# Weight blocks in one tile of five places, neighbours split together, and a fourth pair in blocks in the last down projections

## The chip, the cores and the metric

The kernel runs on one core of one Trainium2 chip. The metric is the device time of one execution in microseconds. A profile of one execution shows what each engine did: TensorE (PE, with its weight loads as PEld), VectorE (DVE), ScalarE (ACT), GpSimd (POOL) and SyncE (SP). SP, ACT and POOL also issue transfers.

## The reference

One layer of a decoder trunk on 256 rows of 2048 floats: a feed-forward block, a mixer (attention beside a matrix memory), an output projection, a second feed-forward block, and a last normalization. All weights are float32, and most of the work is matrix products with them.

```
x = x + 0.5 * swiglu(rmsnorm(x, ffn1_norm), ffn1_w_gate, ffn1_w_up, ffn1_w_down)
h = rmsnorm(x, mix_norm);  parts = split(h @ w_in)
y_a = diff_attention(...);  y_b = mlstm_chunkwise(...) * sigmoid(m_o)
x = x + concat(y_a, y_b) @ w_out
x = x + 0.5 * swiglu(rmsnorm(x, ffn2_norm), ffn2_w_gate, ffn2_w_up, ffn2_w_down)
out = rmsnorm(x, final_norm)
# swiglu(h, g, u, d) = (silu(h @ g) * (h @ u)) @ d ; hidden width 5632
```

## The kernel before, in words

**Products in split precision.** A weight block is cut into a high part `wh` (a cast on ScalarE, line 132) and a low part `wl` (weight minus high part, on VectorE, line 133). Activations are cut the same way. Each product of a 128x128 piece of activations and a 128x512 weight block is then three matmuls (`mms`): two with `wh` (lines 181 and 182) and one with `wl` (line 184). TensorE takes them in the order of the program.

**Pairs in blocks.** The 256 rows are two halves (`hb`). Weights come in tiles of 128 rows by 512 columns, taken in pairs (two tiles down, k and k+1) and, for two neighbouring column chunks `wa` and `wb`, as blocks of two by two. Plainly (`plain`) such a pair takes eight products. A pair "in blocks" takes seven, by a scheme of sums of blocks as in fast matrix multiplication: the class `Paired` does the first `ns` pairs of a product so, and the rest plainly. For each pair in blocks a raw tile of three slots holds the block of `wa` for k (slot 0) and the two of `wb` (slots 1 and 2); the fourth block comes later as `late`. The steps, by their names in the code:

- `leading`: for each two pairs (a "two"; the last may be alone): load, split slot 0 and multiply (A1); then on VectorE the sum T1 writes slots 0 and 1 (line 479). One step later, `second_sum`: split slot 0 and multiply (S1), then T2 adds slot 2 to slot 0: by an accumulating transfer on the POOL queue (line 495) where `by_dma` holds, there are more than three pairs in blocks and the two isn't the last; else on VectorE (line 497).
- `sums`: for each two, load the late block (line 511, SP queue), split slot 0 and multiply (S2), and add the late block to slot 0 by a transfer (line 533, POOL queue); then split and multiply the late blocks themselves (A2, `bare`); then slot 1 (S3).
- `second`: for each pair one split of slots 0 and 2 together (128x1024) for two products, and plain units of `wa` between.
- `third`: the last plain unit of `wa`, then the plain units of `wb`, one for each pair of `rest`. With `last_units` the second half's products of the last units are kept back to the end, so that the first half is finished earlier.

`Chain.run` weaves the leading steps of one product between the `third` steps of the one before.

**Buffers and order.** Raw tiles come from a pool of five (`wr`), plain pairs and late blocks from another five (`rawp`), and `wh` and `wl` from four each. Splits and loads have a high priority in the scheduler that orders each engine's queue; it follows the reads and writes of tiles. `split_weights` also keeps some hand-made order between splits and other work on ScalarE and VectorE. In a `Paired`, block loads go through the POOL queue (lines 446 and 208; SP for the first three chunks of an FFN), plain loads through SP (line 219).

**The feed-forward block.** `ffn` takes the hidden width in groups of 3, 2, 3 and 3 double chunks (`PARTS`). Each group does its gate and up products (5 pairs in blocks of 8; 3 in the second of the first FFN, whose first chunk is taken plainly), and then two down products (chunks 0 and 1, then 2 and 3), each with `NP_DOWN` pairs in blocks: 3, 2, 3 and 3 of 6, 4, 6 and 6. `by_dma` is off for all of them. Hidden pairs that are taken in blocks need their own sums (`sum_pair`, lines 343 to 345, and a split). The mixer's products have 2 pairs in blocks, then 3, 5, 5, 5 and 3; the output projection has two products of 3.

**The end.** The last down product finishes chunk 3 half by half in `store` (from line 1171): add to the residual (line 1181), square on ScalarE (line 300), the last factor (line 1192, POOL), scale (lines 1196 and 1198) and store (line 1199).

Of the kernel before, what the change touches and what calls it, by code (L numbers as in the profile page):

```python
# [9 lines left out]
F32 = mybir.dt.float32  # L10
# [7 lines left out]
P = 128  # L18
# [6 lines left out]
CW = 512  # L25
# [7 lines left out]
UK = 2  # L33
# [5 lines left out]
NP_FIRST = 3  # L39
FIRST_IN = 2  # L40
PARTS = (3, 2, 3, 3)
NP_DOWN = (3, 2, 3, 3)
LK = 4
AHEAD = 400
XLATE = 75
# [4 lines left out]
ON_POOL = 3  # L50
FIRST_SUMS = 3
FLUSH = 3

SEEDED = N11, N21 = "n11", "n21"

# [5 lines left out]
def tile_trunk_layer(ctx: ExitStack, tc: tile.TileContext, x, xt, par, bias_if, lamv, fnorm,  # L61
                     wg1, wu1, wd1, wqk0, wqk1, wqk2, win, wout, wg2, wu2, wd2, out):
    nc = tc.nc
# [1 line left out]
    big = ctx.enter_context(tc.tile_pool(name="big", bufs=1))  # L65
    slots = ctx.enter_context(tc.tile_pool(name="slots", bufs=22))
    work = ctx.enter_context(tc.tile_pool(name="work", bufs=8))
    wr = ctx.enter_context(tc.tile_pool(name="wr", bufs=5))
    wrp = ctx.enter_context(tc.tile_pool(name="wrp", bufs=5))
    wsp = ctx.enter_context(tc.tile_pool(name="wsp", bufs=4))  # L70
    small = ctx.enter_context(tc.tile_pool(name="small", bufs=2))
    ps_acc = ctx.enter_context(tc.tile_pool(name="ps_acc", bufs=4, space=PSUM))
    ps_tr = ctx.enter_context(tc.tile_pool(name="ps_tr", bufs=2, space=PSUM))

    wqk = [wqk0, wqk1, wqk2]
    uid = [0]

    def nm(s):
        uid[0] += 1
        return f"{s}_{uid[0]}"  # L80
# [47 lines left out]
        nc.vector.scalar_tensor_tensor(lo, src, prm[:, gcol:gcol + 1], hi.bitcast(F32),  # L128
                                       op0=ALU.mult, op1=ALU.subtract)

    def split(src, hi, lo):
        return (nc.scalar.copy(hi, src),  # L132
                nc.vector.tensor_tensor(out=lo, in0=src, in1=hi.bitcast(F32), op=ALU.subtract))  # L133


# [1 line left out]
    splits, queued = [], ([], [])  # L137

    def after(late, early):

        tc.add_manual_dep(late.ins, early.ins.name,
                          mybir.DependencyInfo(mybir.DependencyClass.NoSync, mybir.DependencyReason.DATA),
                          reason="order")
# [3 lines left out]

    ahead = ([], [])

    def split_weights(src, hi, lo):  # L150
        made = split(src, hi, lo)
        for late, q, past in zip(made, queued, ahead):
            while q and len(splits) >= q[0][0]:
                past.append(q.pop(0)[1])
            del past[:-3]
            for early in past:
                after(late, early)
        return made


    def pair_tiles(pool, tag, shape):
        return (pool.tile(shape, F32R, tag=tag + "h", name=nm(tag + "h")),
                pool.tile(shape, F32R, tag=tag + "l", name=nm(tag + "l")))
# [36 lines left out]
    def flush(n=None):  # L200

        now = pending[:n]
        del pending[:n]
        for f in now:
            f()

    def load_pair(dst, w, k, queue=nc.sync):
        queue.dma_start(dst, w[k // LK][:, k % LK:k % LK + 2, :])

    def load_unit(w, k, pieces=(UK,), spare=False):  # L210
        n = w.shape[3]
        if spare:
            raw = wr.tile([P, 3, n], F32, tag="raw", name=nm("raw"))[:, 0:UK, :]
        else:
            raw = wrp.tile([P, UK, n], F32, tag="rawp", name=nm("rawp"))
        with tc.high_priority(offset=AHEAD):
            o = k % LK
            for m in pieces:
                nc.sync.dma_start(raw[:, o - k % LK:o - k % LK + m, :], w[k // LK][:, o:o + m, :])
                o += m  # L220
        return raw
# [3 lines left out]
    def in_turn(load):  # L225
        for early in turns[-1:]:
            after(load, early)
        turns.append(load)

    def tile_by_tile(w, ahead):  # L230
        raw = wr.tile([P, 3, w.shape[3]], F32, tag="raw", name=nm("raw"))
        hi, lo = pair_tiles(wsp, "w", [P, UK, w.shape[3]])
        with tc.high_priority(offset=AHEAD):
            for t in range(UK):
                ahead(0, t)
                in_turn(nc.sync.dma_start(raw[:, t, :], w[0][:, t, :]))
                made = split_weights(raw[:, t, :], hi[:, t, :], lo[:, t, :])
        splits.append(made)
        ahead(1)
        return hi, lo  # L240

    def units(accs, xp, w, nk, last_units=1, ahead=None, w0=0, banks=None):
# [16 lines left out]
        for u in range(nu):  # L259
            if u == FLUSH:  # L260
                flush()
# [65 lines left out]
    A1, B1, A2, B2, S3, S1, S2, S4 = range(8)  # L327
# [60 lines left out]
    def gate(src, r):  # L388
        s = wk("sg")
        with soon():  # L390
            ahead_of_splits(0, nc.scalar.activation(s, src, AF.Silu, scale=r))
        return s
# [5 lines left out]
    def soon(extra=40):  # L398
        return tc.high_priority(offset=AHEAD + extra)

    class Early:


        def __init__(self, engine):
            self.engine = engine
# [16 lines left out]
    class Paired:  # L422

        def __init__(self, xp, wa, wb, nk, ns, w0=0, queue=nc.gpsimd, by_dma=True):

            self.queue, self.by_dma = queue, by_dma and ns > 3
            self.xp, self.wa, self.wb, self.k0 = xp, wa, wb, w0 * LK
            self.ns, self.rest = ns, range(2 * ns, nk, UK)
            self.twos = [range(j, min(j + 2, ns)) for j in range(0, ns, 2)]

            self.n = wa.shape[3]
            self.off = self.n - wb.shape[3]
            self.raws = []

        def job(self, acc, j, xi, w, wi, first, last, on=False):
            xh, xl = self.xp[j][2 * (xi // 4):][:2]
# [2 lines left out]

        def load(self, j):  # L440
            n, off = self.n, self.off
            raw = wr.tile([P, 3, n], F32, tag="raw", name=nm("raw"))
            self.raws.append(raw)
            k = self.k0 + 2 * j
            with tc.high_priority(offset=AHEAD):
                self.queue.dma_start(raw[:, 0, :], self.wa[k // LK][:, k % LK, :])
                load_pair(raw[:, 1:3, off:], self.wb, k, self.queue)
                if off:
                    nc.gpsimd.memset(raw[:, 1:3, 0:off], 0.0)

        def split_two(self, srcs):
# [7 lines left out]
                splits.append(made)  # L459
            return t  # L460

        def part(self, js, acc, xi, slot, first=False, last=False):

            t = self.split_two([self.raws[j][:, slot, :] for j in js])
            mms([self.job(acc, j, xi, t, i, first and j == 0, last and j == self.ns - 1, not first)
                 for i, j in enumerate(js)])

# [170 lines left out]
    def ffn(chain, xp, rstd, wg, wu, wd, finish, first=None):  # L638


        def inner(hid, c, ns):
            sg = []

            def half(ag):
                r = rstd()
                sg.extend(gate(ag[hb], r[:, hb:hb + 1]) for hb in range(NT))

            def end(au):
                r = rstd()
                with soon():  # L650
                    hs = [gated(au[hb], r[:, hb:hb + 1], sg[hb]) for hb in range(NT)]
                hid_transposes(hs, hid, c, ns)

            return half, end

        def add(c):
            def run(accs):
                for hb in range(NT):
                    if c % 2:
                        add_half(accs[hb], xres[:, hb, c * CW:(c + 1) * CW], 0.5)  # L660
                    else:
                        add_part(accs[hb], hb, c)

            return run

        done = 0
        for part, (n, ns) in enumerate(zip(PARTS, NP_DOWN)):
            hid = {}
            for c in range(n):
                half, end = inner(hid, c, ns)  # L670
                if done + c == 0 and first is not None:
                    half(linear(xp, wg[0], KD, ahead=first[0],
                                banks=[functools.partial(seeded, b) for b in (N11, N21)]))
                    au = []
                    stream = units(au, xp, wu[0], KD, banks=[bank, bank])
                    for i in range(KD // UK - NP):
                        next(stream)
                        if i < NP_FIRST - FIRST_IN:
                            first[1]()
                    chain.put(stream, NP, functools.partial(end, au))  # L680
                else:
                    np_, queue = NP, nc.sync if done + c < ON_POOL else nc.gpsimd
                    if done + c == 1 and first is not None:
                        np_ = NP_FIRST
                        pending.extend([first[1]] * (NP - NP_FIRST))
                    chain.run(Paired(xp, wg[done + c], wu[done + c], KD, np_, queue=queue), half, end)
            last = part == len(PARTS) - 1
            for c in (0, 2):
                p = Paired(hid, wd[c], wd[c + 1], n * 4, ns, done, by_dma=False)
                if last:  # L690
                    chain.run(p, functools.partial(finish, c), functools.partial(finish, c + 1),
                              LAST_UNITS if c else 1)
                else:
                    chain.run(p, add(c), add(c + 1))
            done += n
# [343 lines left out]
    for hb in range(NT):  # L1039
        for h in range(NH):  # L1040
            i = hb * NH + h
# [226 lines left out]
```

## Time and profile before

| | |
|---|---|
| median of 3 runs | 1759.46 us (1758.83 to 1760.01) |
| the profiled execution's own time | 1759.56 us |
| its span, first to last instruction | 1757.8 us |
| granted TensorE clock | 0.999 |
| instructions | 24486 |
| loads of raw blocks for the gate and up products on POOL | 80 of 256 KB, 80 of 512 KB |

The page gives for each engine its busy time and instructions. Views of the trace group the instructions by line, list waits with who ended them ("A <- B: us in total, times, longest"), follow the chain that ended last, and list instructions in order of time (start, length, engine, line, what is written and read, count).

### The profile page before, as it was taken

The page shows a single profiled execution, that of the slowest core. Times are in us where ns is not written, and L with a number is a line of the kernel's source. Part 1 is how long each engine was busy: PE and PEld are TensorE (multiplying, and loading weights), DVE is VectorE, ACT ScalarE, POOL GpSimd, SP SyncE. Part 2 cuts the span into 40 slices and gives each one's busy share as a digit, 9 for nine tenths or more (in the row PEclk, how much of TensorE's full clock was granted, in tenths as well). Part 3 has the DMA queues.
Part 4 walks back from the last instruction along what each step waited for, and adds up shares of the span by engine and source line. Part 5 has one row for each costly group of instructions (what it writes and reads, how often), then busy time and mean ns, then how long its engine had stood idle before and what let it go on. Part 6 is the DMA issues. An engine that isn't in the chain of part 4 may idle for free.

```text
span 1757.8 us, 24486 instructions
## 1 busy us (share of the span) xinstructions
PE 1744.6 (99%) x7926; PEld 1437.7 (82%) x7926; DVE 1617.8 (92%) x2189; ACT 1267.4 (72%) x1949; POOL 429.3 (24%) x630
## 2 busy tenths in 40 slices
PE   9999999999999999999999999999999999999998
PEld 7788888888888888987888888888888878888886
DVE  7999999999999999898888999999999999999997
ACT  8666777777677768777687777776777677677765
POOL 0022332322233312012231101122332332233310
PEclk9999999999999999999999999999999999999999
DMA  9787998999799977577886667898998999799973
GB/s 365 251 254 209 259 261 265 253 292 265 218 262 258 263 252 204 185 230 221 236 238 192 209 210 211 260 265 233 258 260 268 241 268 276 232 246 256 283 254 115
DMA packets 155265, 429.72 MB, mean 244 GB/s; under 512 B 17632, under 2 KB 18944, under 8 KB 154880
## 3 DMA queue, kind: packets, MB, share of 16 engines
q0 software_dynamic: 76304, 196.66, 45.1%
q1 hardware_dynamic: 77680, 229.40, 38.0%
q10 hardware_dynamic: 1152, 2.09, 0.3%
q8 instruction: 62, 1.02, 0.2%
q14 instruction: 67, 0.55, 0.1%
HBM read 349.56 MB, written 2.10 MB: 200 GB/s over the span
## 4 chain that ended last, share of the span: by engine, by line
PE 93%; DMA 2%; DVE 2%; issue 1%; ACT 0%; POOL 0%; SPq 0%; POOLq 0%; DVEq 0%; ACTq 0%
PE acc L184 18%; PE acc L181 18%; PE acc L182 18%; PE accn L181 12%; PE accn L182 12%; PE accn L184 12%; DVE wl L133 1%; DMA raw<-in_wg_dram 1%; PE tr L373 1%; DMA raw<-in_wu_dram 1%; PE tr L314 0%; PE sc L1060 0%; DMA rawp<-in_wg_dram 0%; ACT wh L132 0%; PE num L1011 0%
## 5 line engine op out<-in xcount | busy, mean ns | idle before, releaser
L132 ACT CAST wh<-raw 128x512 fp32r<-128x512 f32 (+2 forms) x885 | 601.5, 708 | 214.5 <-PE acc L182 66.3
L133 DVE TENSOR_TENSOR wl<-raw,wh 128x512 fp32r<-128x512 f32 (+2 forms) x885 | 676.1, 793 | 58.4 <-ACT wh L132 54.5
L132 ACT CAST wh<-rawp 128x1024 fp32r<-128x1024 f32 (+3 forms) x308 | 318.2, 1035 | 109.5 <-PE acc L182 55.1
L133 DVE TENSOR_TENSOR wl<-rawp,wh 128x1024 fp32r<-128x1024 f32 (+3 forms) x308 | 367.1, 1197 | 32.0 <-ACT wh L132 29.8
L181 PE MATMUL acc<-wh,xs 128*128 128x512 f32 (+2 forms) x956 | 369.5, 387 | 0.0
L182 PE MATMUL acc<-wh,xs 128*128 128x512 f32 (+2 forms) x956 | 368.9, 386 | 0.0
L184 PE MATMUL acc<-wl,xs 128*128 128x512 f32 (+2 forms) x956 | 317.6, 387 | 0.8 <-DVE wl L133 0.7
L533 POOL DMA_DIRECT2D raw<-late x176 | 152.6, 1053 | 442.7 <-DVE wl L133 422.9
L181 PE MATMUL acc<-wh,xt 128*128 128x512 f32 (+2 forms) x564 | 218.4, 388 | 0.7 <-ACT wh L132 0.7
L182 PE MATMUL acc<-wh,xt 128*128 128x512 f32 (+2 forms) x564 | 217.3, 386 | 0.0
L181 PE MATMUL accn<-wh,xt 128*128 128x512 f32 (+1 forms) x552 | 215.3, 391 | 0.0
L182 PE MATMUL accn<-wh,xt 128*128 128x512 f32 (+1 forms) x552 | 214.7, 390 | 0.0
L479 DVE TENSOR_TENSOR raw<-raw 128x1024 f32<-128x1024 f32 x176 | 211.0, 1217 | 0.8
L184 PEld LDWEIGHTS acc<-wl,xs 128*128 128x128 f32 x956 | 178.3, 188 | 39.2 <-DVE wl L133 3.6
L181 PEld LDWEIGHTS acc<-wh,xs 128*128 128x128 f32 x956 | 179.5, 188 | 36.4 <-ACT wh L132 0.6
L182 PEld LDWEIGHTS acc<-wh,xs 128*128 128x128 f32 x956 | 179.6, 188 | 35.6
L181 PE MATMUL accn<-wh,xs 128*128 128x512 f32 (+1 forms) x408 | 162.6, 400 | 1.9 <-ACT wh L132 1.9
L182 PE MATMUL accn<-wh,xs 128*128 128x512 f32 (+1 forms) x408 | 158.0, 388 | 0.0
L184 PE MATMUL acc<-wl,xt 128*128 128x512 f32 (+2 forms) x564 | 157.6, 386 | 0.0
L495 POOL DMA_DIRECT2D raw<-raw x92 | 78.9, 899 | 322.1 <-DVE wl L133 234.7
L184 PE MATMUL accn<-wl,xt 128*128 128x512 f32 (+1 forms) x552 | 154.7, 388 | 0.0
L184 PE MATMUL accn<-wl,xs 128*128 128x512 f32 (+1 forms) x408 | 140.9, 388 | 0.0
(229 smaller groups left out, 2125.0 us busy)
## 6 DMA issues: line engine op xcount, KB each, us to landing
rawp<-in_wd_dram SPq DMA_DIRECT2D x88, 512.0 KB, 5.6
raw<-late POOLq DMA_DIRECT2D x174, 256.0 KB, 5.3
raw<-in_wu_dram POOLq DMA_DIRECT2D x80, 512.0 KB, 8.4
rawp<-in_wu_dram SPq DMA_DIRECT2D x73, 512.0 KB, 5.1
rawp<-in_wg_dram SPq DMA_DIRECT2D x69, 512.0 KB, 5.2
raw<-raw POOLq DMA_DIRECT2D x92, 256.0 KB, 4.1
raw<-in_wd_dram POOLq DMA_DIRECT2D x44, 512.0 KB, 8.6
late<-in_wg_dram SPq DMA_DIRECT2D x41, 512.0 KB, 9.2
```

The lines of the kernel that those rows point to most:

```text
L132: return (nc.scalar.copy(hi, src), nc.vector.tensor_tensor(out=lo, in0=src, in1=hi.bitcast(F32), op=ALU.subtract))
L133: nc.vector.tensor_tensor(out=lo, in0=src, in1=hi.bitcast(F32), op=ALU.subtract))
L181: nc.tensor.matmul(acc, lh, rh, start=first, stop=False, skip_group_check=on)
L182: nc.tensor.matmul(acc, ll, rh, start=False, stop=False, skip_group_check=on)
L184: newest[:] = [nc.tensor.matmul(acc, lh, rl, start=False, stop=last, skip_group_check=on)]
L373: nc.tensor.transpose(tr[:, i, hb * P:(hb + 1) * P], hs[hb][:, k * P:(k + 1) * P], ident)
L479: nc.vector.tensor_tensor(out=raw[:, 0:2, :], in0=raw[:, 0:3:2, :], in1=raw[:, 1:2, :].to_broadcast([P, 2, n]), op=ALU.add)
L495: nc.gpsimd.dma_start(raw[:, 0, :], raw[:, 2, :], accum_op=ALU.add)
L533: nc.gpsimd.dma_start(self.raws[j][:, 0, :], lates[-1][1][:, i, :], accum_op=ALU.add)
```

## The change

Raw blocks no longer come as tiles of a pool, but as places in one tile `ring` of five, dealt in turn (`raw_place`), to `Paired.load` and to the two other users, `load_unit` with `spare` and `tile_by_tile`. Where a two lies in neighbouring places, `part` splits slot 0 (or 1) of both with one cast and one subtraction of 128x1024 (`split_both`); in A1 it makes two casts, one for each block, and one subtraction. Where it doesn't (places 4 and 0, or a lone pair), the split is as before. The last entry of `NP_DOWN` becomes 4, and `by_dma` is on in the last group's two down products of each FFN, so that T2 of their first two goes by transfer.

```
-NP_DOWN = (3, 2, 3, 3)
+NP_DOWN = (3, 2, 3, 4)
+RAWS = 5
...
-    wr = ctx.enter_context(tc.tile_pool(name="wr", bufs=5))
+    wr = ctx.enter_context(tc.tile_pool(name="wr", bufs=1))
...
+    ring = wr.tile([P, RAWS, 3, CW], F32, name="ring")
+    turn = [0]
+    def raw_place():
+        turn[0] += 1
+        return (turn[0] - 1) % RAWS
+    def raw_tile(n):
+        return ring[:, raw_place(), :, 0:n]
...
-    def split(src, hi, lo):
-        return (nc.scalar.copy(hi, src),
+    def split(src, hi, lo, casts=1):
+        for i in range(casts - 1):
+            nc.scalar.copy(hi[:, i:i + 1, :], src[:, i:i + 1, :])
+        return (nc.scalar.copy(hi[:, casts - 1:, :], src[:, casts - 1:, :]) if casts > 1 else nc.scalar.copy(hi, src),
                 nc.vector.tensor_tensor(out=lo, in0=src, in1=hi.bitcast(F32), op=ALU.subtract))
...
-            raw = wr.tile([P, 3, n], F32, tag="raw", name=nm("raw"))
+            place = raw_place()
+            raw = ring[:, place, :, 0:n]
             self.raws.append(raw)
+            self.places.append(place)
...
+        def split_both(self, src, fresh):
+            with tc.high_priority(offset=AHEAD):
+                t = pair_tiles(wsp, "w", [P, 2, self.n])
+                splits.append(split_weights(src, *t, src.shape[1] if fresh else 1))
+            return t
...
-            t = self.split_two([self.raws[j][:, slot, :] for j in js])
+            at = [self.places[j] for j in js]
+            if at[-1] == at[0] + 1:
+                t = self.split_both(ring[:, at[0]:at[0] + 2, slot, 0:self.n], xi == A1)
+            else:
+                t = self.split_two([self.raws[j][:, slot, :] for j in js])
...
-                p = Paired(hid, wd[c], wd[c + 1], n * 4, ns, done, by_dma=False)
+                p = Paired(hid, wd[c], wd[c + 1], n * 4, ns, done, by_dma=last)
```

More of the change, by code (lines that the diff above doesn't have):

```diff
@@ L148, in tile_trunk_layer, with split_weights @@
     ahead = ([], [])
-    def split_weights(src, hi, lo):
-        made = split(src, hi, lo)
+    def split_weights(src, hi, lo, casts=1):
+        made = split(src, hi, lo, casts)
         for late, q, past in zip(made, queued, ahead):
@@ L212, in load_unit @@
         if spare:
-            raw = wr.tile([P, 3, n], F32, tag="raw", name=nm("raw"))[:, 0:UK, :]
+            raw = raw_tile(n)[:, 0:UK, :]
         else:
@@ L230, in tile_by_tile @@
     def tile_by_tile(w, ahead):
-        raw = wr.tile([P, 3, w.shape[3]], F32, tag="raw", name=nm("raw"))
+        raw = raw_tile(w.shape[3])
         hi, lo = pair_tiles(wsp, "w", [P, UK, w.shape[3]])
@@ L432, in __init__ @@
             self.off = self.n - wb.shape[3]
-            self.raws = []
+            self.raws, self.places = [], []
         def job(self, acc, j, xi, w, wi, first, last, on=False):
```

## The prediction, made before the changed kernel was run

> **What bounds the kernel now.** I read the page first: the engines' shares, then the chain that ended last.
>
> ```profile
> span 1757.8 us, 24486 instructions
> ...
> PE 1744.6 (99%) x7926; PEld 1437.7 (82%) x7926; DVE 1617.8 (92%) x2189; ACT 1267.4 (72%) x1949; POOL 429.3 (24%) x630
> ...
> PE 93%; DMA 2%; DVE 2%; issue 1%; ACT 0%; POOL 0%; SPq 0%; POOLq 0%; DVEq 0%; ACTq 0%
> ```
>
> TensorE is busy for 99% of the span and carries 93% of the chain, so what counts is the number of products, and the places where a product waits. VectorE at 92% is the next engine. The chain in order of time gives the price of a product, and the waits of the weight loads say how often VectorE holds one up:
>
> ```profile
> 1671.18 0.91 PE accn L184 x4
> ```
>
> ```profile
> PEld acc L184 <- DVE wl L133: 4.9, 13, 1.0
> ```
>
> Four products of 512 columns in a row take 0.91 us, so one takes 0.2275 us. All waits for the low part of a weight block (wl, which VectorE makes at L133) are 4.9 us together, 13 of them. That is nearly all that a lighter VectorE can give back.
>
> **Fewer products.** A pair of weight tiles taken plainly needs 8 products of three matmuls (two tiles, two column chunks, two halves of the rows), a pair in blocks 7. NP_DOWN's last entry goes from 3 to 4, in two down products in each of two FFNs: four pairs, 4 x 3 = 12 matmuls fewer, 7914 instead of 7926. At 0.2275 us that is **-2.73 us**, all of it on the bounding engine.
>
> **Shared splits.** Places are now dealt in a round of five: four to the first gate chunk, then as many to each block product as it has pairs in blocks. Counted through the program, 65 of the 72 twos lie side by side; the other 7 fall on places 4 and 0. Each shared two makes four subtractions of 128x1024 where there were eight of 128x512, and three casts where there were six (A1 keeps two).
>
> ```profile
> L133 DVE TENSOR_TENSOR wl<-raw,wh 128x512 fp32r<-128x512 f32 x698 | 456.2, 686 | 49.1 <-ACT wh L132 45.4 <-PE acc L184 2.7
> ...
> L133 DVE TENSOR_TENSOR wl<-raw,wh 128x1024 fp32r<-128x1024 f32 x177 | 213.9, 1221 | 9.0 <-ACT wh L132 9.0
> ...
> L132 ACT CAST wh<-raw 128x1024 fp32r<-128x1024 f32 x177 | 185.4, 1054 | 8.4 <-PE acc L182 8.0 <-DMA raw<-in_wg_dram 0.2 <-ACT cv L410 0.2
> ```
>
> By durations a merge saves 2 x 0.686 - 1.221 = 0.15 us. But neighbours on VectorE overlap, as the timeline of VectorE shows where it never pauses:
>
> ```profile
> 650.06 2.35 DVE L479 TENSOR_TENSOR raw<-raw 128x1024 f32<-128x1024 f32 x2
> ...
> 656.52 1.29 DVE L133 TENSOR_TENSOR wl<-raw,wh 128x512 fp32r<-128x512 f32 x2
> ...
> 658.33 0.42 DVE L343 TENSOR_TENSOR xsum<-xg 128x256 f32<-128x256 f32 x1
> ...
> 659.87 0.29 DVE L344 TENSOR_TENSOR xsum<-xsum,xg 128x128 f32<-128x128 f32 x1
> ...
> 660.67 0.28 DVE L345 TENSOR_TENSOR xsum<-xg,xsum 128x128 f32<-128x128 f32 x1
> ...
> 662.61 0.68 DVE L133 TENSOR_TENSOR xs<-xsum,xs 128x512 fp32r<-128x512 f32 x1
> ...
> 666.96 0.69 DVE L133 TENSOR_TENSOR wl<-raw,wh 128x512 fp32r<-128x512 f32 x1
> ...
> 670.49 1.89 DVE L133 TENSOR_TENSOR wl<-raw,wh 128x512 fp32r<-128x512 f32 x3
> ```
>
> Three subtractions of 512 take 1.89 us, so each after the first costs (1.89 - 0.69) / 2 = 0.60; the second of 1024 costs 2.35 - 1.22 = 1.13. A merge therefore frees 2 x 0.60 - 1.13 = 0.07 us of a saturated VectorE. The Trainium skill, "VectorE: DVE Perf Modes", section on the TRN2 errata, says that an instruction on SBUF data pays a fixed cost, which one large tile pays once and many small ones each; its fp32 formula, (N + 151) cycles at 0.96 GHz, gives 0.16 us a merge. That agrees with the durations here, and not with the 0.07 us of this back-to-back row.
>
> TensorE gets of this only what shortens the 13 waits. If each shrinks by one merge, that is 13 x 0.07 = 0.91; nothing if a late load caused them, 4.9 if VectorE's backlog caused all. I take **-0.91**, the low side, because the shared subtraction also ends later for its first block (1.22 against 0.69 after its start).
>
> **The heavier last groups.** Blocks cost VectorE more than plain pairs. From the first loads of a down product to its S3 splits, where neighbours are shared, it does 8 x 1.13 instead of 12 x 0.60 (+1.84), one T1 more (+1.13), one more late block (+0.53), two T2 instead of three (-0.60, see below): +2.90. TensorE has five products more there, 15 x 0.2275 = +3.41. In the first down product of a group come the sums for the fourth hidden pair: 0.42 + 0.29 + 0.28 + 0.68 = +1.67, so VectorE loses 2.90 + 1.67 - 3.41 = 1.16 us on TensorE. In the second the previous product brings one plain unit less (its rest has two units, not three): -1.13 for VectorE, -2.73 for TensorE, so it loses 2.90 - 1.13 - 0.68 = 1.09. What is spare, by stretch (618 to 673 us FFN1's two, from 1676 FFN2's):
>
> ```profile
> core 0: us, PE busy (x) PEld busy (x) DVE busy (x) ACT busy (x) POOL busy (x), PEclk, DMA share, GB/s
> 618.00:648.00 30.00, 30.00 (x138) 24.81 (x137) 28.34 (x35) 20.75 (x30) 6.54 (x11) 1.00 0.81 252
> 648.00:673.00 25.00, 25.00 (x116) 20.38 (x115) 24.33 (x39) 20.04 (x37) 2.61 (x3) 1.00 0.58 171
> ...
> 1676.00:1707.00 31.00, 31.00 (x142) 25.64 (x141) 28.72 (x36) 21.59 (x31) 3.75 (x5) 1.00 0.78 241
> 1707.00:1749.00 42.00, 42.00 (x187) 34.53 (x185) 38.40 (x57) 26.54 (x45) 3.34 (x4) 1.00 0.37 107
> ```
>
> VectorE has 1.66, 2.28 and 3.60 us free in the first, third and fourth: enough. The second, FFN1's last down product, has 0.67, and there the lead is already gone:
>
> ```profile
> 667.70 0.50 PE L184 MATMUL acc<-wl,xs 128*128 128x512 f32 x1
> ```
>
> The subtraction that began at 666.96 ended at 667.65, and its product started at 667.70. Here the second two also wraps (places 4 and 0), which costs 8 x 0.60 - 4 x 1.13 = 0.28 more: 1.09 + 0.28 = **+1.37 us** of TensorE waiting (0 if VectorE comes into it further ahead than now; 2.5 if the first down product's 1.16 is added).
>
> **T2 by transfer.** In each of the four, the first two's T2 becomes two transfers. They leave VectorE (2 x 0.60, counted above) and go to the POOL queue, behind them the late additions (L533) and the next product's loads.
>
> ```profile
> L495 POOL DMA_DIRECT2D raw<-raw x92 | 78.9, 899 | 322.1 <-DVE wl L133 234.7 <-DMA late<-in_wg_dram 51.5 <-DMA raw<-in_wu_dram 25.0
> ```
>
> ```profile
> raw<-raw POOLq DMA_DIRECT2D x92, 256.0 KB, 4.1
> ```
>
> ```profile
> ACT wh L132 <- DMA raw<-raw: 6.6, 14, 1.2
> ```
>
> ```profile
> 661.54 0.62 PE L184 MATMUL acc<-wl,xs 128*128 128x512 f32 x2
> ```
>
> S1's subtractions of the first two end at X = 657.81 (656.52 + 1.29). The second transfer lands 0.90 + 4.1 = 5.0 later; cast 1.05 and subtraction 1.22 make X + 7.3. TensorE reaches S1's low part at 661.54 = X + 3.73, then two products, S1 of the other two (6), a plain unit (12) and four high ones, 24 x 0.2275 = 5.46: it needs the block at X + 9.2. So I take **0**; four times the longest wait seen, 4 x 1.2 = 4.8, is the upper end, and below nothing it can't go, since VectorE's gain is counted. The Trainium skill, "DMA: Bandwidth & Descriptors", section on the anatomy of a SWDGE DMA, gives 2.0 us plus bytes / 436e3, 2.6 us for 256 KB, an estimate from that page; the row has 4.1, and the sum goes by the row.
>
> **The end.** The last product keeps back its second row half for LAST_UNITS = 3 units; now only two are left.
>
> ```profile
> 1745.20 0.76 DVE L1181 SCALAR_TENSOR_TENSOR xres<-acc,xres 128x256 f32<-128x256 f32 x2 [1.53 <-PE acc L184]
> ...
> 1747.78 0.92 DVE L1198 TENSOR_SCALAR xres<-xres,rstd 128x544 f32<-128x544 f32 x2 [0.47 <-POOL rstd L1192]
> ...
> 1748.50 0.94 ACTq L1199 DMA_DIRECT2D out_dram<-xres  x2
> ...
> 1749.28 0.76 DVE L1181 SCALAR_TENSOR_TENSOR xres<-acc,xres 128x256 f32<-128x256 f32 x2 [0.59 <-PE acc L184]
> 1749.74 0.42 ACT L300 ACTIVATE junk<-xres 128x256 bf16<-128x256 f32 x1 [0.68 <-DVE xres L1181]
> ```
>
> The halves are 4.08 us apart (18 products); they will be 12 x 0.2275 = 2.73 apart. The first half keeps VectorE until 1748.70 (3.50 after its start) and ScalarE, which issues its stores, until 1749.44 (4.24). The second half's square would start at 2.73 + 0.46 = 3.19, but ScalarE is free only at 4.24. **+1.05 us** if the order of the queues stays; 0 if the second half is put ahead of the first one's stores.
>
> **Free edits.** One tile for all places costs nothing if dependences follow regions, not the tile. The trace has such a case:
>
> ```profile
> 643.30 0.74 POOL L208 DMA_DIRECT2D raw<-in_wqk_dram  x1
> 644.02 0.14 POOL L449 MEMSET raw<- 128x16 f32 x1
> ```
>
> ```profile
> raw<-in_wqk_dram POOLq DMA_DIRECT2D x2, 384.0 KB, 6.3
> ```
>
> The memset writes columns 0 to 7 of the two rows whose other columns the transfer fills. The two regions interleave, and it ran at once, 6 us before the landing. POOL gets 8 transfers, and for the four extra pairs 12 loads and late additions that SP's plain loads did before, each some 0.9 us: 18 us in all, in its 76% idle time. ScalarE, 72% busy, has casts taken away.
>
> **Sum.** The profiled execution took 1759.56: -2.73 - 0.91 + 1.37 + 0 + 1.05 = -1.22, so 1758.3. The runs' median is 0.10 below it: **1758.2**.
>
> **The rivals.** *Relief* (faster): VectorE's backlog caused the waits, so all 4.9 us go, FFN1's end doesn't stall, and the second half is put first: 1759.46 - 2.73 - 4.9 = 1751.8, or 1753 with the end as above. For it: a product with two shared twos has 6 merges ahead of its S2 matmuls, by durations 6 x 0.15 = 0.9 us of lead, near the longest wait (1.0). Against it: back to back they are 6 x 0.07 = 0.42. By the Trainium skill's fixed cost, named above, it would be this one.
>
> *Later of two loads* (slower): A1's one subtraction now waits for both blocks' loads and casts.
>
> ```profile
> ACT wh L132 <- DMA raw<-in_wg_dram: 42.4, 31, 3.6
> ```
>
> Where the second load is late, the first block's 0.60 us is no longer done meanwhile. It decides where the lead is under 0.60: at the 13 waits at most, 7.8 us, so 1766.0. Against it: most A1 splits lead by more, as S1 does above.
>
> *T2 late*: 4.8 us, 1763.0. Against it stands the margin of 1.9 us.
>
> *Whole-tile dependences*: each of the 45 block products would expose a load, some 6 us by the row of 6.3, over 270 us, 2030. The memset speaks against it.
>
> **Numbers.** Chances: forecast 0.57 (own range 1755.9 to 1761.5), relief 0.22, later load 0.10, T2 late 0.08, whole tile 0.03. 0.2% is 3.5 us, about what a measurement of this kernel can tell from no change. Faster by that: relief, 0.22. Slower: later load, whole tile and a little of T2, 0.15. The rest 0.63. The range runs from 1753.0, into relief, to 1763.5, past T2; outside lie the later load, the whole tile and relief's far end.
>
> **What would show it.** Right: 7914 matmuls; some 240 fewer instructions on VectorE; waits of L184 loads for L133 near 4 us in the old places and about 1.4 us new near 665 us; 2.7 us between the two L1181 groups that end the kernel, and ScalarE's square late after the second. Wrong: long waits of casts for raw<-raw, new waits for wl behind A1, or loads that wait for splits of other places.

## The result, and the profile after

The changed kernel takes 1814.01 us (median of 6 runs, 1811.35 to 1817.05) against 1760.19 beside it (6 runs): the ratio is 1.0306, with a 95% interval from 1.0292 to 1.0320. It is 53.8 us slower; the prediction was 1758.2, no difference. The page of the profiled execution, and its rows of waits and of groups:

```profile
span 1809.8 us, 23985 instructions
...
PE 1770.3 (98%) x7914; PEld 1434.9 (79%) x7914; DVE 1612.1 (89%) x1949; ACT 1254.0 (69%) x1770; POOL 443.5 (25%) x650
...
PE 76%; DMA 10%; DVE 7%; issue 4%; ACT 2%; POOL 0%; SPq 0%; DVEq 0%; POOLq 0%; ACTq 0%
```

```profile
ACT wh L147 <- DMA ring<-ring: 55.4, 35, 5.9
PEld acc L199 <- DVE wl L148: 30.2, 61, 1.4
PEld acc L196 <- ACT wh L147: 21.9, 19, 3.2
```

```profile
L148 DVE TENSOR_TENSOR wl<-ring,wh 128x1024 fp32r<-128x1024 f32 x437 | 529.9, 1221 | 112.2 <-ACT wh L147 103.3 <-PE accn L197 4.9 <-PE acc L199 2.1
```

Lines have moved: 147 is the cast (132 before), 148 the subtraction (133), 196, 197 and 199 the matmuls (181, 182, 184), 523 T2 by transfer (495), 531 the copy of a sum (503), 561 the late addition (533), 1209, 1226 and 315 the lines 1181, 1198 and 300 of the end. The counts are as foretold: 7914 matmuls, 240 instructions fewer on VectorE, and 437 - 177 = 260 = 4 x 65 merged subtractions. But TensorE carries 76% of the chain instead of 93%, and transfers 10%. ScalarE's casts wait 55.4 us for transfers within the tile (6.6 before), and behind them TensorE waits for low parts 30.2 us (4.9 before) and for high parts 21.9. VectorE has less to do than before, and TensorE still waits for it six times as long. What VectorE itself waits for stands in the L148 row: of its 112.2 us idle before subtractions of 128x1024, 103.3 end with ScalarE's cast.

The timeline of FFN1's first down product of the last group shows how:

```profile
643.72 2.51 DVE L148 TENSOR_TENSOR wl<-ring,wh 128x1024 fp32r<-128x1024 f32 x2
...
645.24 1.76 POOL L523 DMA_DIRECT2D ring<-ring  x2 [11.75 <-DVE wl L148]
...
645.97 0.61 PE L199 MATMUL acc<-wl,xs 128*128 128x512 f32 x2
...
652.33 1.04 ACT L147 CAST wh<-ring 128x1024 fp32r<-128x1024 f32 x1 [5.93 <-DMA ring<-ring]
...
653.43 0.50 PE L196 MATMUL acc<-wh,xs 128*128 128x512 f32 x1 [2.76 <-ACT wh L147]
```

The first of the two subtractions of the 643.72 row is S1 of a shared two. When it ends (1.22 later, 644.94), both T2 transfers are released, and POOL issues them in one go, 645.24 and 645.80. They land one after the other, at 648.59 and 652.23. S2's shared cast needs both, so ScalarE stands idle for 5.93 us, and TensorE for 2.76. The chain that ended last holds such transfers in several more places, two pieces of it for instance:

```profile
1494.75 9.27 DMA ring<-ring x2
...
1598.72 12.31 DMA ring<-ring x2
```

These two lie in FFN2's gate and up products, which the prediction's part on T2 didn't look at.

### The profile page after: what moved, and what is told of

Read it like the earlier page. It is cut to its first block, busy times and chain, and to the rows that moved or that the text cites. A ratio compares the mean times of both kernels' runs of the same rounds, so it can differ in the third digit from the quotient of the medians.

```text
span 1809.8 us, 23985 instructions
## 1 busy us (share of the span) xinstructions
PE 1770.3 (98%) x7914; PEld 1434.9 (79%) x7914; DVE 1612.1 (89%) x1949; ACT 1254.0 (69%) x1770; POOL 443.5 (25%) x650
## 4 chain that ended last, share of the span: by engine, by line
PE 76%; DMA 10%; DVE 7%; issue 4%; ACT 2%; POOL 0%; SPq 0%; DVEq 0%; POOLq 0%; ACTq 0%
PE acc L199 15%; PE acc L196 14%; PE acc L197 14%; PE accn L196 10%; PE accn L197 10%; PE accn L199 10%; DVE wl L148 5%; DMA ring<-ring 5%; DMA ring<-in_wg_dram 3%; ACT wh L147 1%; DVE ring L507 1%; PE tr L388 1%; DMA ring<-in_wu_dram 1%; DMA ring<-in_wd_dram 1%; DMA xraw<-in_xt_dram 0%
## 5 line engine op out<-in xcount | busy, mean ns | idle before, releaser
L148 DVE TENSOR_TENSOR wl<-ring,wh 128x1024 fp32r<-128x1024 f32 (+2 forms) x645 | 667.2, 1051 | 121.9 <-ACT wh L147 111.8
L147 ACT CAST wh<-ring 128x512 fp32r<-128x512 f32 (+2 forms) x645 | 554.3, 872 | 243.7 <-DMA ring<-ring 55.4
L196 PE MATMUL acc<-wh,xs 128*128 128x512 f32 (+2 forms) x976 | 380.7, 391 | 15.0 <-ACT wh L147 13.5
L148 DVE TENSOR_TENSOR wl<-rawp,wh 128x1024 fp32r<-128x1024 f32 (+3 forms) x300 | 357.0, 1195 | 27.5 <-ACT wh L147 25.9
L197 PE MATMUL acc<-wh,xs 128*128 128x512 f32 (+2 forms) x976 | 378.4, 388 | 0.0
L199 PE MATMUL acc<-wl,xs 128*128 128x512 f32 (+2 forms) x976 | 329.1, 394 | 2.1 <-DVE wl L148 0.9
L561 POOL DMA_DIRECT2D ring<-late x180 | 155.6, 1055 | 435.1 <-DVE wl L148 397.5
L507 DVE TENSOR_TENSOR ring<-ring 128x1024 f32<-128x1024 f32 (+1 forms) x180 | 214.1, 1217 | 1.7
L196 PE MATMUL acc<-wh,xt 128*128 128x512 f32 (+2 forms) x548 | 212.6, 389 | 0.7 <-ACT wh L147 0.7
L197 PE MATMUL acc<-wh,xt 128*128 128x512 f32 (+2 forms) x548 | 211.4, 386 | 0.0
L196 PE MATMUL accn<-wh,xt 128*128 128x512 f32 (+1 forms) x536 | 209.0, 391 | 0.0
L197 PE MATMUL accn<-wh,xt 128*128 128x512 f32 (+1 forms) x536 | 208.1, 389 | 0.0
L523 POOL DMA_DIRECT2D ring<-ring x100 | 86.6, 1010 | 373.5 <-DVE wl L148 356.4
```

Source lines behind the costliest of these rows:

```text
L147: return (nc.scalar.copy(hi[:, casts - 1:, :], src[:, casts - 1:, :]) if casts > 1 else nc.scalar.copy(hi, src), nc.vector.tensor_tensor(o ...
L196: nc.tensor.matmul(acc, lh, rh, start=first, stop=False, skip_group_check=on)
L197: nc.tensor.matmul(acc, ll, rh, start=False, stop=False, skip_group_check=on)
L199: newest[:] = [nc.tensor.matmul(acc, lh, rl, start=False, stop=last, skip_group_check=on)]
L507: nc.vector.tensor_tensor(out=raw[:, 0:2, :], in0=raw[:, 0:3:2, :], in1=raw[:, 1:2, :].to_broadcast([P, 2, n]), op=ALU.add)
L523: nc.gpsimd.dma_start(raw[:, 0, :], raw[:, 2, :], accum_op=ALU.add)
```

## The experiments

Theory: a shared split of S1 or S2 **releases** together what two splits released one by one, the two T2 transfers and the two late additions, and a shared S2 also waits for both; that, not VectorE's time, makes the stalls. Rivals: whole-tile dependences; A1's single subtraction; a long subtraction that stands badly in VectorE's queue; VectorE's load in the last groups. Each kernel was compared with the kernel before on the same chip.

| kernel | us | ratio to before, 95% interval |
|---|---|---|
| tile alone | 1761.57 | 1.0005 [0.9995, 1.0015] |
| tile and all shared splits, three pairs | 1792.45 | 1.0179 [1.0164, 1.0194] |
| all shared but A1 | 1798.10 | 1.0193 [1.0157, 1.0228] |
| all shared but S1 | 1781.26 | 1.0112 [1.0090, 1.0135] |
| all shared but S2 | 1777.96 | 1.0094 [1.0073, 1.0115] |
| only S3 shared | 1762.84 | 1.0008 [0.9997, 1.0018] |
| only S1 shared | 1775.03 | 1.0084 [1.0069, 1.0099] |
| only S2 shared | 1773.42 | 1.0072 [1.0053, 1.0092] |
| nothing shared, T2 transfers reversed | 1791.52 | 1.0177 [1.0153, 1.0201] |
| nothing shared, late additions reversed | 1766.03 | 1.0032 [1.0019, 1.0044] |
| all shared, one transfer for two | 1793.85 | 1.0193 [1.0173, 1.0214] |
| fourth pair, T2 by transfer, no tile | 1774.52 | 1.0077 [1.0062, 1.0092] |
| fourth pair, T2 on VectorE, no tile | 1778.84 | 1.0096 [1.0079, 1.0112] |
| fourth pair in the first down product only | 1768.09 | 1.0041 [1.0026, 1.0056] |
| fourth pair in the second only | 1766.58 | 1.0037 [1.0024, 1.0049] |
| fourth pair in both, without T1 | 1765.29 | 1.0029 [1.0019, 1.0038] |
| changed kernel, T2 of last groups on VectorE | 1803.24 | 1.0238 [1.0216, 1.0260] |
| changed kernel, only A1 and S3 shared | 1775.29 | 1.0088 [1.0071, 1.0105] |

### The parts by themselves

The first kernel has the tile `ring`, the pool's old counts and every split as before (`if False:` in place of `if at[-1] == at[0] + 1:`, with NP_DOWN and by_dma as before); the second adds the shared splits; the third is the kernel before with the other half of the change, the fourth the same with T2 on VectorE:

```
-NP_DOWN = (3, 2, 3, 3)
+NP_DOWN = (3, 2, 3, 4)
...
-                p = Paired(hid, wd[c], wd[c + 1], n * 4, ns, done, by_dma=False)
+                p = Paired(hid, wd[c], wd[c + 1], n * 4, ns, done, by_dma=last)
```

> The places of the ring alone: no shared splits, three pairs in blocks in the last group, T2 there on VectorE. If the ring's dependences or its fixed order of places delay loads, most of the 54 us stay (over 20 us). If sharing and the fourth pair are the cause, the time is that of the kernel before within 2 us.

> Ring and shared splits, three pairs in blocks in the last group, T2 there on VectorE. The stalls by product in the changed trace give the gate and up products about 30 us and the last groups' down products 22: if sharing is what delays the gate and up products, this run is about 27 to 32 us over the kernel before; if the fourth pair and its transfers alone are the cause, it is the kernel before within 3 us.

> The kernel before (pool of five tiles, no sharing) with the fourth pair and T2 by transfer. If the transfer is late by itself, TensorE stalls some 5 us or more in each first down product of a last group, 10 to 20 us over the kernel before. If it is late only because the shared S1 split releases both transfers at once, it comes out 0 to 3 us faster than the kernel before.

> The kernel before with the fourth pair, T2 on VectorE as in the other down products. 12 matmuls fewer are 2.7 us; four T2 more on VectorE than with transfers, at 0.60 each, in stretches where VectorE is full. If transfers cause the stalls of the last groups: 0 to 2.7 us faster than the kernel before. If the fourth pair itself overloads VectorE: 5 us slower or more.

The tile costs nothing: dependences follow its places. Sharing costs 31.7 us, the fourth pair 13.7, together 45.4 of the 53.8. The third kernel's time fits the expectation for transfers that are late by themselves, but the fourth has none of these transfers and is no faster, so it is the pair that costs. Where nothing is shared, T2 by transfer is 4.3 us better by the medians than on VectorE; the two intervals overlap, so it is no worse, and that it is better is not shown. The waits of the kernel with shared splits and three pairs have the pattern of the changed kernel:

```profile
ACT wh L147 <- DMA ring<-ring: 33.8, 27, 5.2
PEld acc L199 <- DVE wl L148: 27.8, 57, 2.0
PEld acc L196 <- ACT wh L147: 14.3, 16, 2.7
```

### Which shared split

One condition is changed in `part`, in the kernel with all shared splits and three pairs (with `!= A1`, `!= S1`, `!= S2`, `== S3`, `== S1`, `== S2` in turn):

```
-            if at[-1] == at[0] + 1:
+            if at[-1] == at[0] + 1 and xi != A1:
```

> Like e2_share_only (31.7 us over the kernel before), but A1 split block by block as before. If A1's single subtraction, which waits for the later of two loads, is the cause: within 8 us of the kernel before. If the later steps (S1, S2) are, because they send their transfers late and together: still 20 us or more over it.

> Like e2_share_only, but S1 split block by block. The two T2 transfers of a two are then issued apart (1.7 us in the kernel before, 0.5 in the changed one). If their coming together delays S2, and so the loads behind it: at most 12 us over the kernel before. If A1 is the cause, or S2: 20 us or more over it.

> Like e2_share_only, but S2 split block by block. If S2's shared split sends the two late additions late, so that the buffers of the late blocks come free late and the plain loads of SP run into the block loads of POOL: at most 12 us over the kernel before. If A1 or S1 is the cause: 20 us or more over it.

> Ring, and only S3's splits shared; S3 waits for no transfer and sends none. If sharing costs by what waits for it and what it sends: the kernel before within 3 us. If every shared split costs by its longer latency alone (cast and subtraction of 1024 end later for the first block): a quarter of the 31.7 us, some 8 us.

> One tile, and only S1's neighbours share a split (no A1, S2, S3), three pairs. Taking S1's sharing away from all four gave back 11.2 us (1792.45 to 1781.26). If its harm stands by itself, S1 alone costs 9 to 14 us: 1770 to 1775, and the waits of casts for ring<-ring grow from about 7 to 25 us or more. If it only hurts in company with S2's (the two delays add up past a margin), S1 alone stays under 1765.

> One tile, and only S2's neighbours share a split, three pairs. Taking S2's sharing away from all four gave back 14.5 us (1792.45 to 1777.96). If its harm stands by itself, S2 alone costs 12 to 17 us: 1773 to 1778, and SP's loads that wait for the late additions start 1 to 2 us later in each product. If it only hurts in company with S1's, it stays under 1766.

A1 doesn't do it by itself: without its sharing the kernel is no faster (1798.10 against 1792.45). S3 costs 1.3 us over the tile alone (1762.84 against 1761.57), no more than can be measured. S1 and S2 each cost by themselves, 13.5 and 11.9 us over the tile alone, and give 11.2 and 14.5 back when taken from the four. Both release a transfer that another engine waits for; A1 and S3 don't.

If one of them were the cause alone, the kernel without its sharing was to be at most 12 us over the kernel before; it is 20.3 over without S1's and 17.0 without S2's, so both have a part. Their single costs make 25.4 of the 30.9 us that all sharing costs over the tile alone; the other 5.5 are not put down to a step. With A1, S2 and S3 shared the kernel is 7.8 us slower than with S2 alone (1781.26 against 1773.42), so A1 or S3 may cost in company; no run shows that by itself.

The waits with S1 alone shared, then with S2 alone:

```profile
ACT wh L147 <- DMA ring<-ring: 22.1, 22, 2.5
PEld acc L196 <- ACT wh L147: 12.7, 11, 1.9
PEld acc L199 <- DVE wl L148: 7.9, 20, 1.5
```

```profile
ACT wh L147 <- DMA ring<-ring: 21.8, 20, 3.1
PEld acc L199 <- DVE wl L148: 13.9, 34, 1.4
PEld acc L196 <- ACT wh L147: 5.4, 9, 1.2
```

The tile alone has 6.8 us for the casts, 3.2 for the high parts and 4.5 for the low parts (its rows stand below). With S1 shared TensorE waits above all for high parts, which no subtraction of VectorE makes. With S2 shared it waits more for low parts; whether the cast that needs two landings or the longer subtraction makes these late, the runs don't separate.

### Released together, without any shared split

The sharpest test takes the tile alone and makes only the order on the POOL queue other, so that the first transfer of a two waits behind the second; every other queue has the order of the tile alone:

```
-                for j in js:
-                    raw = self.raws[j]
+                made = []
+                for raw in [self.raws[j] for j in (js[::-1] if self.by_dma and js != self.twos[-1] else js)]:
                     if self.by_dma and js != self.twos[-1]:
-                        nc.gpsimd.dma_start(raw[:, 0, :], raw[:, 2, :], accum_op=ALU.add)
+                        made.append(nc.gpsimd.dma_start(raw[:, 0, :], raw[:, 2, :], accum_op=ALU.add)); made[1:] and after(made[1], made[0])
```

The other kernel does the same to the late additions of a two in the products of 512 columns, most of the mixer's among them (the output projection's first is left out). In the mixer, at 751 us, VectorE and POOL each also swap a small neighbouring instruction once.

> One tile, no shared split at all, three pairs, every instruction of every engine as in the kernel with the tile alone (1761.6). Only the two T2 transfers of a two change their order on the POOL queue: the second pair's first, so the first pair's waits behind it and both are released together, as a shared S1 releases them. Theory 'released together' (the pair of transfers lands late since they start together): the casts' waits for ring<-ring grow from 7 to 25 us or more, and the time to 1769 to 1775. Rival 'the queue of VectorE' (the long merged subtraction stands behind T1 and ends late for its first block): nothing changes, 1760 to 1763.

> One tile, no shared split, three pairs; only the late additions of a two change their order on the POOL queue (products of 512 columns outside the mixer): both are released together after the second S2 split. If S2's harm comes from its releasing the late additions late and together, 1767 to 1775, with SP's plain loads 0.5 us and more later. If it comes from the shared cast, which waits for both T2 transfers, nothing changes here: 1760 to 1763.

Nothing is shared, VectorE and ScalarE do the same work, and yet 30.0 us are lost over the tile alone. That is over twice what S1's sharing costs (13.5), and beyond the 1769 to 1775 expected; that it comes near the 30.9 of all shared splits is chance, for nothing of S2 is in it. The reversed order is harsher than a shared split: the block that S2 takes first now lands last, and the casts wait 50.6 us for transfers, against 22.1 with S1 shared. So the run shows that a late release of these transfers is enough to cost tens of microseconds, not how much of the 30.9 it is. First the waits of the tile alone, then those with the order reversed:

```profile
ACT wh L147 <- DMA ring<-ring: 6.8, 12, 1.5
PEld acc L199 <- DVE wl L148: 4.5, 13, 1.2
PEld acc L196 <- ACT wh L147: 3.2, 5, 1.1
```

```profile
ACT wh L147 <- DMA ring<-ring: 50.6, 36, 4.2
PEld acc L196 <- ACT wh L147: 25.3, 25, 2.6
PEld acc L199 <- DVE wl L148: 12.5, 32, 1.6
```

One two in FFN2's second gate and up product, in the timeline of the tile alone:

```profile
1110.07 0.84 POOL L523 DMA_DIRECT2D ring<-ring  x1 [1.16 <-DVE wl L148]
...
1111.81 0.86 POOL L523 DMA_DIRECT2D ring<-ring  x1 [0.90 <-DVE wl L148]
...
1116.03 0.62 ACT L147 CAST wh<-ring 128x512 fp32r<-128x512 f32 x1 [0.69 <-DMA ring<-ring]
...
1117.29 0.62 ACT L147 CAST wh<-ring 128x512 fp32r<-128x512 f32 x1 [0.16 <-DMA ring<-ring]
```

And the same two with the order reversed (its product runs some 14 us later):

```profile
1126.08 1.73 POOL L523 DMA_DIRECT2D ring<-ring  x2 [2.56 <-DVE wl L148]
...
1134.41 0.62 ACT L147 CAST wh<-ring 128x512 fp32r<-128x512 f32 x1 [4.18 <-DMA ring<-ring]
...
1135.08 0.50 PE L196 MATMUL acc<-wh,xs 128*128 128x512 f32 x1 [1.98 <-ACT wh L147]
```

One by one the transfers are issued 1.74 us apart, and the casts wait 0.69 and 0.16 us for them (15 of the 46 twos of the tile alone are issued 0.6 us apart even so). Together they go out at 1126.08 and 1126.62, the first pair's lands last, at 1134.31, and the cast of its block waits 4.18 us. The place of a long subtraction in VectorE's queue is not needed for it: that rival falls as the main cause of what S1 costs. The late additions, reversed, cost 4.5 us (1766.03 against 1761.57), between the two ranges expected; so of S2's 11.9 they are a part, and the rest fits its shared cast's wait for two landings, which no run shows apart.

Does a pair land late for its bytes, or for what each transfer costs? The last kernel of this group has all shared splits and makes one transfer of 512 KB out of two, for T2 and for the late additions:

```
+                at, n = [self.places[j] for j in js], self.n
+                one = self.by_dma and js != self.twos[-1] and at[-1] == at[0] + 1
+                if one:
+                    nc.gpsimd.dma_start(ring[:, at[0]:at[0] + 2, 0, 0:n], ring[:, at[0]:at[0] + 2, 2, 0:n], accum_op=ALU.add)
```

> All shared splits, three pairs (1792.45), but the two T2 transfers of a shared two are one transfer of 512 KB, and its two late additions too: half the issues on POOL, the same bytes, released at the same time. If the second transfer lands late because the DMA engines move the bytes one after the other (6.4 us after the release), one transfer lands no earlier: 1788 to 1796. If a fixed share of each transfer and its issue makes it late, one transfer lands 1 to 2 us earlier, and much of the 31.7 us goes: 1765 to 1780.

```profile
ring<-ring POOLq DMA_DIRECT2D x34, 512.0 KB, 5.6
ring<-ring POOLq DMA_DIRECT2D x24, 256.0 KB, 4.3
```

It is no better (1793.85), as the first expectation had it (its 6.4 us is counted from the second transfer's own issue; from the release it is 7.3). Yet the one transfer does land sooner: 5.6 us after its issue, where in the kernel with two the second landed 6.3 us after the issue of the first (median of the 38 twos issued less than 0.7 us apart, from the trace's issues and landings). These 0.7 us gain nothing that can be measured, and nothing can start at its half; so bytes and a fixed share are not told apart. The Trainium skill, "DMA: Bandwidth & Descriptors", section on the anatomy of a SWDGE DMA, would give 2.6 and 3.2 us by its formula, an estimate; these rows have 4.3 and 5.6, twice as much for each 256 KB more.

### The fourth pair

In the kernel before with the fourth pair (no tile), `ns - (last and c == 2)` keeps three pairs in the second down product, `c == 0` in the first; the third of these kernels leaves T1 out where there are four pairs (`for j in js if self.ns != 4 else ():`).

> No tile, no shared split. The fourth pair with T2 by transfer only in the first down product of the two last groups; the second keeps three pairs. Six matmuls fewer: -1.4 us. If each product bears its own stalls as they lie in the kernel with both (first products 2.2 and 1.8 us, of which the fourth hidden pair's sums 1.3 and 0.9), 1762 to 1765. If the first product's load is what pushes the second (its backlog carried on), 1768 to 1773.

> No tile, no shared split. The fourth pair with T2 by transfer only in the second down product of the two last groups; the first keeps three. If each product bears its own stalls as in the kernel with both (second products 4.5 and 2.9 us, and 4.6 us behind FFN1's, less 1.4 for six matmuls), 1769 to 1773. If they were carried on from the first product, 1760 to 1764.

> Fourth pair with T2 by transfer in both, no shared split (1774.5), and T1 is left out in these four products (the additions L479 that make the operands of S1, S3 and S4; the output is not the reference's): VectorE does 4 x 1.13 = 4.5 us less in each, more than the 2.9 us that the fourth pair brought. If the stalls come from VectorE's load, the time falls under that of before by up to the 2.7 us of the 12 matmuls: 1758 to 1762. If they come from chains that VectorE's load doesn't set (the hidden pair's sums behind the gate, transfers, loads of wd, places that come free late), it stays at 1768 or more.

The first costs 7.2 us, the second 5.6, nearly the 13.7 of both: each bears its own. But neither time lies in its range for that (1768.09 is above it, in the other range, and 1766.58 below it), so I had split them wrongly. Without T1 VectorE is busy 17.0 us less (1612.1 against 1629.1), and 9.2 of the 13.7 come back, again between the two ranges. T1 is also a step between A1 and S1, so that leaving it out shortens this chain as well as the load; the run doesn't separate the two. And 4.4 us stay, and the 2.7 of the matmuls are still not seen, so load isn't all. In the first product a single chain shows, in the timeline of the kernel with the fourth pair in both:

```profile
635.05 0.74 DVE L395 SCALAR_TENSOR_TENSOR sg<-acc,rstd,sg 128x512 f32<-128x512 f32 x1
635.71 0.28 DVE L345 TENSOR_TENSOR xsum<-hg,xsum 128x128 f32<-128x128 f32 x1
...
636.03 0.62 ACT L132 CAST xs<-xsum 128x512 fp32r<-128x512 f32 x1 [0.82 <-DVE xsum L345]
...
636.70 0.50 PE L181 MATMUL acc<-wh,xs 128*128 128x512 f32 x1 [1.10 <-ACT xs L132]
```

The fourth hidden pair's sums stand behind the gate of the last hidden chunk (L395) on VectorE; the first product that takes them waits 1.10 us for their cast. The table of stretches shows that VectorE has time left there, and in the next stretch none:

```profile
618.00:648.00 30.00, 28.80 (x128) 22.85 (x127) 26.61 (x37) 20.09 (x31) 5.41 (x7) 1.00 0.78 227
648.00:673.00 25.00, 22.53 (x102) 17.69 (x100) 24.60 (x37) 18.87 (x33) 6.25 (x12) 1.00 0.69 211
```

With the fourth pair in the second product alone, the next product (the mixer's first) waits for its plain loads: TensorE loses 3.0 us in two places at 713 and 717 us (idle time between matmuls beyond their usual distance). ScalarE's row in the timeline:

```profile
712.32 0.83 ACT L132 CAST wh<-rawp 128x768 fp32r<-128x768 f32 x1 [2.74 <-DMA rawp<-in_wqk_dram]
```

Four of the five places are then taken, where three pairs left two free: the next product has two pairs in blocks, whose loads went out at 642.77 and 645.04 before; now the first goes at 645.80 and the second at 679.82, among the loads of the product after it. That this is what holds up the plain loads was not tried by itself.

### The two together

> The changed kernel with T2 of the last groups left on VectorE; shared splits and the fourth pair as in it. Without sharing that cost 4.3 us more (1778.84 against 1774.52). If in the changed kernel the two transfers that a shared S1 releases together make the last groups' stalls (20 us there), this kernel is faster than the changed one: 1802 to 1809. If VectorE's load makes them, it is slower: 1816 to 1822.

> The changed kernel, but only A1 and S3 share their splits; the tile of five places, the fourth pair and T2 by transfer as in it. If all that sharing costs, in the gate and up products and in the last groups, comes from S1 and S2, what is left is the fourth pair's 13.7 us: 1772 to 1776. If the rest of the changed kernel's 54 us (54 - 31.7 - 13.7 = 8) comes from other sharing in the last groups, 1780 or more.

The first of these is the changed kernel with `by_dma=False`, the second the changed kernel with `xi not in (S1, S2)` added to the condition of sharing. With A1 and S3 shared alone, what is left is the fourth pair's cost (1775.29 against 1774.52 without tile or sharing). So the other 39 us of the changed kernel, the 8 that the parts didn't add up to among them, all go through S1 and S2. And T2 by transfer, no loss without sharing, is a loss of 10.8 us with it (1814.01 against 1803.24). The waits of ScalarE and TensorE in FFN1's first down product of the last group, 640 to 668 us of the changed kernel:

```profile
PEld acc L196 <- ACT wh L147: 3.2, 1, 3.2
```

```profile
ACT wh L147 <- DMA ring<-ring: 5.9, 1, 5.9
```

With T2 on VectorE neither row is there in that product. No version beat the kernel before.

## Why the prediction was wrong, point by point

**Fewer products.** The count was right, 7914. No run shows the 2.73 us as a gain, since every kernel with a fourth pair lost more.

**Shared splits.** The step that failed. 65 shared twos were counted, and 65 are there. A merge was to free 0.07 us of VectorE; in the kernel with shared splits and three pairs VectorE is busy 1604.7 us against 1617.5 with the tile alone, over 204 merges 0.063 each. That was right too. Wrong was "TensorE gets of this only what shortens the 13 waits", -0.91 us: I asked what the merged instruction takes and what it waits for, and not who waits for it. S1 ends the reading of slot 0 and so releases T2, S2 the late addition. The measured cost is +31.7 us, with three pairs, in products that I didn't cost at all: ScalarE's casts wait 33.8 us for the transfers there, and the waits for low parts, which were to shrink, went from 4.9 to 27.8 us.

**Heavier last groups.** +1.37 against +13.7 and the 2.7 that didn't come, some 16 us. I weighed VectorE's time over stretches of 25 to 42 us; the stalls came from single late steps in them, too, as the hidden sums, and from a product behind the group.

**T2 by transfer.** Taken as 0, at most 4.8, and only for the four new products. The working let the second transfer land at X + 5.0, as if it were alone. In the changed kernel X is 644.94, the second landed at 652.23, X + 7.3, and TensorE reached S1's low part at X + 1.0 and not at X + 3.73. The lost lead alone doesn't make the stall: with only A1 and S3 shared, in the same product, TensorE came at X + 0.2 (X is 633.31 there), but the two transfers went out 1.74 us apart, the second landed at 637.12, X + 3.8, and S2's high parts didn't wait. What failed is the landing of a pair that starts together. The rival "T2 late" had the right mechanism. Its place and price were wrong, since the 92 transfers of the products that had it already are released by shared splits as well.

**The end.** +1.05 was worked out. From the start of the last matmul to the end of the span it is 8.97 us before and 10.58 after: +1.6. That the size is near is luck: the halves are 3.60 us apart, not 2.73, and VectorE is what stands in the way, not ScalarE:

```profile
1799.61 0.92 DVE L1226 TENSOR_SCALAR xres<-xres,rstd 128x544 f32<-128x544 f32 x2 [0.47 <-POOL rstd L1220]
1800.51 0.41 DVE L1209 SCALAR_TENSOR_TENSOR xres<-acc,xres 128x256 f32<-128x256 f32 x1
...
1801.31 0.42 ACT L315 ACTIVATE junk<-xres 128x256 bf16<-128x256 f32 x1 [0.43 <-DVE xres L1209]
```

The second half's residual stands behind the first half's scaling, and ScalarE is idle 0.43 us before its square.

**One tile.** Right: 1.0005 [0.9995, 1.0015]. The rival "whole-tile dependences" falls, and "later of two loads" (A1) with it as the main cause; what A1 costs in company is open. "Relief" falls too: with less work on VectorE the waits that it was to empty grew.

What would have warned me was in the trace of before, in a row that I quoted: casts already waited 14 times, 6.6 us in all, for these transfers. I read it as a small price; it also says that in 14 places a transfer that lands later makes ScalarE later by as much.

## What to carry to other kernels

Before two instructions are merged, list who is released by each of them: what the first one let go now goes with the second, and of what then starts together (here two transfers of 256 KB) the second ends later. A wait behind a transfer in the trace of before, however short, marks where to look for that. Where a group gets heavier, follow the one chain that is due last in each product; a mean over 25 us doesn't show it.

## What the chip showed beside that

Two accumulating transfers of 256 KB within on-chip memory that POOL issues together land one behind the other. The pair shown, issued 0.56 us apart, landed 3.35 and 6.43 us after their own issue; over the 47 twos of the changed kernel issued less than 0.7 us apart the medians are 4.0 and 5.9, and one transfer of 512 KB took 5.6 at the median. How much of that is the load that other queues put on the transfers, no run shows. Merging two subtractions of 512 columns saved VectorE 0.063 us of busy time. And what an edit is worth depends on its company: T2 by transfer cost nothing in one kernel and 10.8 us in the other.
